# One PSUM bank moved from the transpose pool to the projection pool of a hybrid attention kernel

## Chip, core and metric

The kernel runs on one core of a Trainium2 chip, in one launch. The metric is the time on the device in microseconds (us). TensorE is called PE below, VectorE DVE, ScalarE ACT, GpSimd POOL; SyncE (SP) issues the transfers. [...]

## What is computed

One block with two branches over 2048 tokens of width 1024, float32, cut to what matters:

```python
h = rmsnorm(x, norm_g)
proj = einsum("bsd,de->bse", h, w_in)
glu_in, conv_gate, q, k, v, attn_gate, merge_logits = split(proj, SPLIT_POINTS)
c = conformer_conv(glu_in, ...)        # a * sigmoid(b), 31 taps per channel, layernorm, silu
y_conv = (c * silu(conv_gate)) @ w_conv_out
q, k = rope(q), rope(k)                # 16 query heads, 4 key heads of 64
a = sliding_window_attention(q, k, v, sinks)     # window 128
y_attn = (a * silu(attn_gate)) @ w_attn_out
g_conv, g_attn = split(sigmoid(merge_logits))
x = x + (g_conv * y_conv + g_attn * y_attn) @ w_out
return rmsnorm(x, final_norm_g)
```

## The kernel before

The tokens go through in two sweeps of 1024 (`sweep`). Activations lie transposed in SBUF (channels on partitions), each as a high and a low half of reduced precision, and a product is the sum of three: high by high, high by low, low by high.

`project` (L267) makes an item: one block of 128 output channels for the two halves of 512 tokens of the sweep. `load_w` (L244) fetches the weight block in two parts: a transfer into `raw`, a cast on ACT into `whi` (L253), and the low part `wlo` as a subtraction on POOL (L242, `split_lo`), or in the second sweep as a transfer of the stored low part. Per half, 24 matmuls (8 blocks of input channels by 3) go into one PSUM tile `mm_<name>` from the pool `mm_ps` (L276). `evac` then reads that tile out, with a raised priority (L284, L285): items gb by a sigmoid on ACT (L415), ga by a product on DVE (L419), the gates cg, ag, ma and mc on ACT (L434), q and k by four rope products on DVE (L460, L461 of item a, L466, L467 of item b), whose sums POOL makes (L468, L469) and ACT splits (L296), v on ACT (L519). A tile's bank is free for a later tile when its last reader has ended.

The pool `tp_ps` holds the tiles of transposes and of weighted values, one bank each: tpf (`build_h_first`, the transposed first activations, 8 tiles for each half of the first sweep; read by ACT at L363 and by DVE at L364), tpx (`build_h`, the second sweep), tpv (values, L497; read by ACT at L501 and L513 and by DVE at L502, L503 and L242), tpp (probabilities of the attention, L592, read by ACT at L599 and by DVE) and ov (weighted values, L610, read by ACT at L617 and DVE at L618). [...] 

The order of PE is the program's own: it is written out by hand, with the class `Line` placing attention steps, value transposes and convolution taps between the blocks of the projection items. The other engines are put in order by a scheduler that goes by priorities and by when it thinks operands are ready. The convolution's 31 taps for each of 8 channel blocks and each sweep run on DVE (L389, L393, 128x1024 each) beside the projections. The first sweep begins with tpf, gb and ga of the first block, k, v and q (to about 220 us), goes on with gb, ga and gates, and has the attention among them up to about 630 us; then come the gates ma and mc, the output projections, and the second sweep.

Of the kernel before, what the change touches and what calls it, by code (L numbers as in the profile page):

```python
# [53 lines left out]
def hybrid_block(ctx: ExitStack, tc: tile.TileContext, x, par_d, w_in, w_conv, sinks, w_attn, w_out,  # L54
# [5 lines left out]
    slots = ctx.enter_context(tc.tile_pool(name="slots", bufs=1))  # L60
    stage = ctx.enter_context(tc.tile_pool(name="stage", bufs=4))
    work = ctx.enter_context(tc.tile_pool(name="work", bufs=2))
    mm_ps = ctx.enter_context(tc.tile_pool(name="mm_ps", bufs=3, space=bass.MemoryType.PSUM))
    tp_ps = ctx.enter_context(tc.tile_pool(name="tp_ps", bufs=3, space=bass.MemoryType.PSUM))
    sc_ps = ctx.enter_context(tc.tile_pool(name="sc_ps", bufs=1, space=bass.MemoryType.PSUM))
    dram = ctx.enter_context(tc.tile_pool(name="dram", bufs=1, space=bass.MemoryType.DRAM))

# [889 lines left out]
```

## Time and profile before

| what | us |
|---|---|
| median of 3 runs | 2091.1 (2090.81 to 2091.75) |
| profiled execution, its own time | 2090.34 |
| its span, first to last instruction | 2088.4 |
| PE busy | 2044.0 |
| DVE busy | 1391.3 |
| ACT busy | 1032.4 |
| POOL busy | 483.2 |
[...]

The span is the profiled execution without 1.9 us around it. PE is busy for all but 44 us of it, and all its idle time of more than a trifle lies before 632 us. Three ways of reading the trace are used below. The waits of an engine name, for idle time, the line that sat idle and the instruction that ended the idleness. Busy time by stretch shows which engine has no idle time in a part of the span, and the clock that was granted there. The timeline lists single instructions or runs of equal ones, with the idle time ahead of each in brackets.

### The profile page before, as it was taken

What the parts mean: (1) busy time and instruction counts of PE and PEld (TensorE: products, weight loads), DVE (VectorE), ACT (ScalarE), POOL (GpSimd) and SP (SyncE); (2) the same over time, 40 slices, a digit from 0 to 9 for tenths busy, and PEclk for the clock granted to TensorE, in tenths of its full rate; (3) what the DMA queues carried; (4) which work ended last, traced back from release to release, by engine and by line L of the source; (5) the groups of instructions that cost most, each with busy time, mean ns of one, the idle gap of its engine ahead of it and who ended that gap; (6) DMA issues with size and microseconds to landing.
All of it is one profiled execution on the core that took longest, in us unless ns stands there. A gap on an engine that the chain in (4) does not pass through costs nothing.

```text
span 2088.4 us, 27452 instructions
## 1 busy us (share of the span) xinstructions
PE 2044.0 (98%) x9256; PEld 1671.7 (80%) x9256; DVE 1391.3 (67%) x1901; ACT 1032.4 (49%) x2265; POOL 483.2 (23%) x336
## 2 busy tenths in 40 slices
PE   7999999998999999999999999999999999999998
PEld 6787888886777888888888888888888888888887
DVE  4979779998988348123559596698888934341324
ACT  6221377666667646112442214766777774621222
POOL 2445433433334222243001131121111110000200
PEclk9999999999999999999999999999999999999999
DMA  7344555554455775646344456555555578574432
GB/s 250 133 144 157 178 166 157 158 163 146 148 152 182 254 238 184 202 142 221 101 151 132 141 161 204 172 158 175 175 163 164 175 225 259 162 236 146 140 119 81
DMA packets 265820, 355.90 MB, mean 170 GB/s; under 512 B 28112, under 2 KB 126544, under 8 KB 265680
## 3 DMA queue, kind: packets, MB, share of 16 engines
q1 hardware_dynamic: 265680, 354.16, 53.3%
q8 instruction: 73, 1.20, 0.2%
q14 instruction: 67, 0.55, 0.1%
HBM read 234.51 MB, written 119.54 MB: 170 GB/s over the span
## 4 chain that ended last, share of the span: by engine, by line
PE 70%; DVE 4%; issue 2%; ACT 1%; DMA 0%; POOL 0%; SPq 0%; DVEq 0%; POOLq 0%; ACTq 0%
PE o L877 9%; PE mm_mc L281 8%; PE mm_yc L281 8%; PE mm_ya L281 8%; PE mm_ma L281 7%; PE mm_ga L281 5%; PE mm_cg L281 5%; PE mm_ag L281 4%; PE mm_gb L281 4%; DVE cv L393 2%; PE mm_q_a L281 2%; PE mm_q_b L281 2%; PE ov L614 2%; PE sc L566 2%; PE mm_v L281 1%
## 5 line engine op out<-in xcount | busy, mean ns | idle before, releaser
L393 DVE SCALAR_TENSOR_TENSOR cv<-glu,par,cv 128x1024 f32<-128x1024 f32 x480 | 675.9, 1408 | 6.7
L605 POOL TENSOR_SCALAR_AFFINE_SELECT pc<-pt 128x1024 fp32r<-128x1024 f32 x60 | 102.7, 1711 | 452.9 <-DVE pt L242 419.6
L877 PE MATMUL o<-wo,mT 128*128 128x512 f32 x768 | 181.3, 394 | 0.0
L877 PEld LDWEIGHTS o<-wo,mT 128*128 128x128 f32 x768 | 143.1, 188 | 32.1
L281 PE MATMUL mm_cg<-hT,whi_cg 128*128 128x512 f32 x512 | 163.2, 400 | 4.6 <-ACT glu L415 3.0
L281 PE MATMUL mm_ma<-hT,whi_ma 128*128 128x512 f32 x512 | 162.9, 399 | 4.0 <-ACT whi_ma L253 4.0
L281 PE MATMUL mm_ga<-hT,whi_ga 128*128 128x512 f32 x512 | 161.0, 395 | 0.2 <-ACT whi_ga L253 0.2
L281 PE MATMUL mm_ag<-hT,whi_ag 128*128 128x512 f32 x512 | 160.9, 395 | 0.0
L281 PE MATMUL mm_gb<-hT,whi_gb 128*128 128x512 f32 x512 | 160.6, 395 | 0.0
L281 PE MATMUL mm_mc<-hT,whi_mc 128*128 128x512 f32 x512 | 159.6, 393 | 0.0
L281 PE MATMUL mm_yc<-uT,whi_yc 128*128 128x512 f32 x512 | 159.4, 392 | 0.0
L281 PE MATMUL mm_ya<-aT,whi_ya 128*128 128x512 f32 x512 | 158.7, 391 | 0.0
L281 PEld LDWEIGHTS mm_cg<-hT,whi_cg 128*128 128x128 f32 x512 | 95.3, 191 | 25.2 <-ACT glu L415 3.4
L281 PEld LDWEIGHTS mm_ma<-hT,whi_ma 128*128 128x128 f32 x512 | 95.1, 190 | 23.9 <-ACT whi_ma L253 4.4
L281 PEld LDWEIGHTS mm_yc<-uT,whi_yc 128*128 128x128 f32 x512 | 96.2, 188 | 21.9
L281 PEld LDWEIGHTS mm_mc<-hT,whi_mc 128*128 128x128 f32 x512 | 96.0, 188 | 21.8
L281 PEld LDWEIGHTS mm_ya<-aT,whi_ya 128*128 128x128 f32 x512 | 96.1, 188 | 20.9
L281 PEld LDWEIGHTS mm_ga<-hT,whi_ga 128*128 128x128 f32 x512 | 94.5, 188 | 20.8 <-ACT whi_ga L253 1.0
L281 PEld LDWEIGHTS mm_gb<-hT,whi_gb 128*128 128x128 f32 x512 | 94.7, 188 | 20.0
L281 PEld LDWEIGHTS mm_ag<-hT,whi_ag 128*128 128x128 f32 x512 | 94.2, 188 | 19.7 <-ACT whi_ag L253 0.3
L584 ACT ACTIVATE ss<-ss,st 128x128 f32<-128x128 f32 x256 | 99.9, 391 | 19.2 <-DVE st L579 18.6
L815 POOL TENSOR_TENSOR lmc<-lmc,mp 128x512 f32<-128x512 f32 x32 | 41.9, 1309 | 275.5 <-DVE lmc L814 267.1
(363 smaller groups left out, 4356.4 us busy)
## 6 DMA issues: line engine op xcount, KB each, us to landing
qk<-d_q SPq DMA_DIRECT2D x256, 64.0 KB, 2.7
d_a<-ss SPq DMA_DIRECT2D x128, 128.0 KB, 1.9
aT<-d_a SPq DMA_DIRECT2D x32, 512.0 KB, 6.1
qk<-d_k SPq DMA_DIRECT2D x240, 64.0 KB, 2.1
raw_gb<-in_w_in_dram SPq DMA_DIRECT2D x34, 256.0 KB, 4.0
raw_ga<-in_w_in_dram SPq DMA_DIRECT2D x34, 256.0 KB, 3.4
raw_ag<-in_w_in_dram SPq DMA_DIRECT2D x32, 256.0 KB, 3.8
d_ag<-ag SPq DMA_DIRECT2D x32, 256.0 KB, 2.1
```

What stands on the lines that cost most here:

```text
L281: pe.matmul(out=ps, lhsT=a, rhs=b, start=(k == 0 and i == 0), stop=(k == KC - 1 and i == 2))
L393: dve.scalar_tensor_tensor(out=cv[c], in0=glu[c][:, j:j + T], scalar=tap(c, j), in1=cv[c], op0=ALU.mult, op1=ALU.add)
L566: pe.matmul(out=o, lhsT=q[:, h, :], rhs=r, start=(j == 0), stop=(j == 1))
L584: act.activation(out=sb[:, h, :], in_=sb[:, h, :], func=AF.Exp, scale=SCALE, bias=ngm[:, h:h + 1], accum_out=den[:, h:h + 1])
L605: pool.affine_select(out=pc, in_=f(pt), pattern=[[0, 2], [0, GQ], [1, P]], compare_op=ALU.is_ge, fill=0.0, base=0, channel_multiplier=-1)
L614: pe.matmul(out=ov, lhsT=vv, rhs=pp[:, i % 2], start=(i == 0), stop=(i == nm - 1))
L815: pool.tensor_tensor(out=g, in0=g, in1=mp[e][:, half * TH:(half + 1) * TH], op=ALU.add)
L877: pe.matmul(out=ps, lhsT=a[:, c0:c0 + P], rhs=r, start=(k == 0 and i == 0), stop=(k == KC - 1 and i == 2))
```

## The change

The pool of projection tiles gets four buffers instead of three, the pool of transposes and weighted values two instead of three. Nothing else is edited.

```diff
-    mm_ps = ctx.enter_context(tc.tile_pool(name="mm_ps", bufs=3, space=bass.MemoryType.PSUM))
-    tp_ps = ctx.enter_context(tc.tile_pool(name="tp_ps", bufs=3, space=bass.MemoryType.PSUM))
+    mm_ps = ctx.enter_context(tc.tile_pool(name="mm_ps", bufs=4, space=bass.MemoryType.PSUM))
+    tp_ps = ctx.enter_context(tc.tile_pool(name="tp_ps", bufs=2, space=bass.MemoryType.PSUM))
```

In both kernels the tiles of a pool take its banks in turn. The order of PE and POOL is the same instruction for instruction; DVE, ACT and SP differ only in the first 35 us or so. On ACT, at the start, hT is the copy of a tpf tile, sqf the square of an input block of the second half, whi the cast of a weight block:

```order
 L363 ACTIVATE hT_0_2_126<-tpf_2_192,par 128x512
-L363 ACTIVATE hT_0_3_127<-tpf_3_199,par 128x512
 L253 CAST whi_gb_000_139<-raw_gb_000_137 128x512
 L253 CAST whi_gb_001_145<-raw_gb_001_143 128x512
+L363 ACTIVATE hT_0_3_127<-tpf_3_199,par 128x512
 L363 ACTIVATE hT_0_4_128<-tpf_4_206,par 128x512
+L350 ACTIVATE sqf_0_235,ssf_234<-xf_0_149 128x1024
 L363 ACTIVATE hT_0_5_129<-tpf_5_213,par 128x512
-L350 ACTIVATE sqf_0_235,ssf_234<-xf_0_149 128x1024
-L363 ACTIVATE hT_0_6_130<-tpf_6_220,par 128x512
 L351 ACTIVATE ssf_234<-ssf_234,eps_t 128x1
 L350 ACTIVATE sqf_1_240,ssf_234<-xf_1_151 128x1024
```

The copies of tiles 3, 5 and 6 now stand behind two casts and one square each. The last copy has moved further, behind all four squares:

```order
-L363 ACTIVATE hT_0_7_131<-tpf_7_227,par 128x512
+L363 ACTIVATE hT_0_6_130<-tpf_6_220,par 128x512
 L351 ACTIVATE ssf_234<-ssf_234,eps_t 128x1
 L350 ACTIVATE sqf_2_245,ssf_234<-xf_2_153 128x1024
 L350 ACTIVATE sqf_3_250,ssf_234<-xf_3_155 128x1024
 L351 ACTIVATE ssf_234<-ssf_234,eps_t 128x1 x2
+L363 ACTIVATE hT_0_7_131<-tpf_7_227,par 128x512
 L253 CAST whi_ga_000_257<-raw_ga_000_255 128x512
```

On PE the order stands, and what an instruction waits for changes. At the third tile of transposed values (tpv_1_0; vs is the ACT copy of the projected values) before had

```order
L281 MATMUL mm_v_792<-hT_1_7_320,whi_v_665 128x512 x2
L281 MATMUL mm_v_792<-hT_1_7_320,wlo_v_666 128x512
L281 MATMUL mm_q_a_858<-hT_0_0_124,whi_q_a_730 128x512 x2
L281 MATMUL mm_q_a_858<-hT_0_0_124,wlo_q_a_731 128x512 [waits Pool_49]
L499 MATMUL tpv_1_0_862<-ident_r,vs_1_0_790 128x128 [waits Activation_49]
L499 MATMUL tpv_1_0_862<-ident_r,vs_1_0_790 128x128 x3
```

and after has

```order
L281 MATMUL mm_v_792<-hT_1_7_320,whi_v_665 128x512 x2
L281 MATMUL mm_v_792<-hT_1_7_320,wlo_v_666 128x512
L281 MATMUL mm_q_a_858<-hT_0_0_124,whi_q_a_730 128x512 x2
L281 MATMUL mm_q_a_858<-hT_0_0_124,wlo_q_a_731 128x512 [waits Pool_49]
L499 MATMUL tpv_1_0_862<-ident_r,vs_1_0_790 128x128 [waits DVE_49]
L499 MATMUL tpv_1_0_862<-ident_r,vs_1_0_790 128x128 x3
```

The wait for ACT has become one for DVE: the tile takes the bank of the first tpv tile, whose last reader is on DVE (L242).

## Rows read from the trace of the kernel before

**Rows 1.** Waits of PE: engine, tile, line, releaser: us, times, longest.

```profile
PE mm_ma L281 <- ACT whi_ma L253: 4.0, 1, 4.0
PE mm_q_b L281 <- DVE rb_q__1_1524 L467: 3.4, 1, 3.4
...
PE mm_cg L281 <- ACT glu L415: 3.0, 1, 3.0
...
PE mm_cg L281 <- ACT cg L434: 1.7, 1, 1.7
...
PE mm_q_b L281 <- DVE ra_q__0_1408 L461: 1.3, 1, 1.3
...
PE mm_q_b L281 <- DVE ra_q__0_1579 L461: 0.5, 1, 0.5
```

**Rows 2.** Stretches: length, busy time of each engine, granted clock, DMA share, GB/s.

```profile
139.00:213.00 74.00, 68.78 (x290) 55.13 (x289) 72.84 (x61) 10.38 (x18) 33.57 (x21) 0.98 0.45 143
...
636.00:2086.00 1450.00, 1445.64 (x6537) 1186.16 (x6535) 854.73 (x1250) 687.12 (x1499) 237.36 (x164) 1.00 0.55 174
...
91.80:96.00 4.20, 2.09 (x12) 1.81 (x12) 4.20 (x8) 2.53 (x7) 0.00 (x0) 1.00 0.00 0
198.83:202.24 3.41, 3.41 (x9) 2.63 (x9) 3.27 (x3) 1.29 (x3) 2.71 (x2) 0.50 0.48 150
...
628.91:635.74 6.83, 5.72 (x13) 3.93 (x14) 6.77 (x8) 3.78 (x9) 4.72 (x3) 0.50 0.21 47
```

The engines stand in the order PE, weight load of PE, DVE, ACT, POOL.

**Rows 3.** Waits of DVE from 235 to 632 us, as in rows 1.

```profile
DVE st L586 <- ACT ss L584: 15.5, 9, 4.8
...
DVE glu L419 <- PE mm_ga L281: 4.9, 1, 4.9
```

**Rows 4.** Timeline of PE at the start: start, us, instruction, idle before.

```profile
11.77 5.84 PE L361 MATMUL tpf<-ident_r,xf 128*128 128x128 f32 x25 [0.89 <-DVE xf L354]
18.11 0.66 PE L361 MATMUL tpf<-ident_r,xf 128*128 128x128 f32 x4 [0.50 <-DVE hT L364]
18.52 0.70 PE L281 MATMUL mm_gb<-hT,whi_gb 128*128 128x512 f32 x2
...
24.45 0.73 PE L281 MATMUL mm_ga<-hT,whi_ga 128*128 128x512 f32 x2 [0.21 <-ACT whi_ga L253]
25.87 0.50 PE L281 MATMUL mm_ga<-hT,wlo_ga 128*128 128x512 f32 x1 [0.70 <-POOL wlo_ga L242]
```

**Rows 5.** Timeline of DVE at the start.

```profile
13.01 2.46 DVE L364 SCALAR_TENSOR_TENSOR hT<-tpf,par,hT 128x512 fp32r<-128x512 f32 x3 [1.29 <-ACT hT L363]
```

**Rows 6.** Timeline of ACT at the start.

```profile
12.28 0.69 ACT L363 ACTIVATE hT<-tpf,par 128x512 fp32r<-128x512 f32 x1 [1.55 <-PE tpf L361]
...
15.55 1.13 ACT L253 CAST whi_gb<-raw_gb 128x512 fp32r<-128x512 f32 x2
...
17.73 1.06 ACT L350 ACTIVATE sqf<-xf 128x1024 f32<-128x1024 f32 x1
```

**Rows 7.** Timeline of PE, later places.

```profile
93.93 0.66 PE L499 MATMUL tpv<-ident_r,vs 128*128 128x128 f32 x4 [2.11 <-ACT vs L519]
...
223.22 0.62 PE L281 MATMUL mm_ga<-hT,whi_ga 128*128 128x512 f32 x2
223.68 0.39 PE L281 MATMUL mm_ga<-hT,wlo_ga 128*128 128x512 f32 x1
...
502.44 0.60 PE L594 MATMUL tpp<-ident_r,ss 128*128 128x128 f32 x4
```

**Rows 8.** Timeline of DVE, later places.

```profile
95.68 0.42 DVE L242 TENSOR_TENSOR vt<-tpv,vt 128x256 fp32r<-128x256 f32 x1
...
138.60 0.69 DVE L419 TENSOR_TENSOR glu<-mm_ga,glu 128x512 f32<-128x512 f32 x1 [4.90 <-PE mm_ga L281]
```

**Rows 9.** Timeline of POOL around 220 us.

```profile
219.09 1.30 POOL L242 TENSOR_TENSOR wlo_ga<-raw_ga,whi_ga 128x512 fp32r<-128x512 f32 x1 [1.30 <-issue]
```

**Rows 10.** Timeline of ACT in the attention.

```profile
519.30 0.58 ACT L599 CAST pt<-tpp 128x512 fp32r<-128x512 f32 x1
```

## The prediction, made before the changed kernel ran

> **What bounds the kernel now.** I read the waits of TensorE (PE) first, because PE has little idle time to give back: whatever the change brings must be one of those waits. The rows to look at are the five in which a projection tile (an "mm" tile) waits for the reader of an older mm tile: VectorE (DVE) rope lines L467 and L461, ScalarE (ACT) lines L415 and L434. They come to 3.4 + 1.3 + 0.5 = 5.2 us in the rope stretch and 3.0 + 1.7 = 4.7 us in the attention stretch [rows 1]. These are true buffer waits: the reader holds the tile three back, which is the bank that the next tile wants. The row for mm_ma (4.0 us, for the cast of a weight block, at the end of the attention stretch) is not one; a buffer does nothing for it.
>
> Then the busy time by stretch. From 139 to 213 us DVE is busy 72.84 of 74 us, more than PE. [...] From 636 us on PE is busy 1445.64 of 1450 us: it alone sets the pace there, and a shift of the 632 us before stays a shift of the end [rows 2].
>
> Last, who paces 235 to 632 us. The waits of DVE there have one row for PE, 4.9 us, and all others for ACT, 15.5 us ahead [rows 3]. So DVE and ACT run a chain of their own that PE doesn't hold up, and PE is their customer.
>
> **The change part by part: two transpose buffers at the start.** The order of PE and of GpSimd (POOL) stays word for word. Each of the eight tpf tiles takes four transposes of 0.234 us, 0.93 us in all (5.84 us for 25) [rows 4], then an ACT copy and a DVE subtraction that ends the tile's life. On DVE three of these took 2.46 us, so 0.75 us and some for each [rows 5]; the ACT copy is 0.69 us [rows 6]. With three buffers PE lost 0.50 us once, before the last tile at 18.11 [rows 4]. With two, tile k+2 starts when DVE has done with tile k: 0.93 + 0.69 + 0.75 and two hand-overs, some 2.5 us for two tiles, where PE alone needs 1.9. Besides, ACT's order now has the two weight casts (1.13 us) ahead of hT3 and the 1.06 us square ahead of hT5 [rows 6], as the order of the changed kernel shows. Walking through: tile 2 at 13.8, tile 3 at 14.7, tile 4 at 16.4 (behind hT2 on DVE), tile 5 at 18.0 (hT3 behind the casts), tile 6 at 18.9, tile 7 at 20.5 (hT5 behind the square); mm_gb begins at about 21.3 instead of 18.52, +2.8. hT7 now stands behind all four squares on ACT and comes free of DVE at about 26.1, just ahead of mm_gb's last three matmuls at 26.3. Against this, PE lost 0.21 + 0.70 us at the next item, mm_ga, waiting for weights, with 0.11 twice in slower first matmuls, a pair in 0.73 and a single in 0.50 [rows 4], where 0.62 and 0.39 are usual [rows 7]; a later PE finds those weights there: −1.1. So +1.7 at full clock. The clock rose at about 17.9 before. With gaps between the transposes it rises with mm_gb or one stretch of 3.4 us later: 0 to 1.6 us; I take the middle, 0.8. Sum: +2.5, bounds 1.7 and 5.
>
> **Two transpose buffers at the value tiles.** At 93.93 the third tpv tile waited 2.11 us for ACT's copy of its input [rows 7]. With two buffers it takes the bank of the first tpv tile, whose last reader, DVE's L242, ends at 95.68 + 0.42 = 96.10 [rows 8]. That is 2.2 us later; queued behind the transpose on PE is the whole of mm_q_a, so all of it is lost. The idle becomes 4.3 us, and the two rows of half clock follow idles of 3.4 and 4.0 us; a stretch of 3.41 us at half clock costs 1.7. Sum: +3.9, bounds 2.2 and 5.1 (5.8 us at half clock). The two costs pass on: DVE waited 4.90 us for PE at 138.60, right ahead of its saturated stretch [rows 8], so it starts that stretch as late as PE does.
>
> [...] Without any cost of clock the sum would be the second rival's.
>
> **A fourth projection buffer, rope stretch.** It removes the 5.2 us, and the stretch of half clock behind the 3.4 us (1.7 us). But PE then comes 6.9 us earlier to mm_ga, which it met at 223.22, with the low half of the weights at 223.68 [rows 7]. That low half is POOL's at 219.09 to 220.39 [rows 9], behind ACT's cast of the same weights. Both stand behind the last step of the rope chain of the saturated DVE, which a buffer doesn't speed up. So PE gets 223.68 − 220.39 = 3.3 us, about 3.2 with the hand-over, and the rest turns into idle there, 3.7 us in two parts. Such an idle may halve the clock: 0 to 1.7, and I take half, 0.8. Gain: 2.4, bounds 1.5 and 3.2. What PE gains it passes on, since DVE waits for PE 4.9 us more, for the second half of this mm_ga [rows 3].
>
> **A fourth projection buffer, attention stretch.** The 4.7 us go as PE waits, but the end of the stretch is the cast of whi_ma that mm_ma waits for [rows 1], at the end of the DVE and ACT chain. PE would wait there for as much longer. Cost and gain nothing; if the chain were not the limit, −4.7 and −1.7 for the clock (third rival).
>
> **Two transpose buffers in attention.** Five tpp and ov tiles, from 442 to 506 us, start there before the last reader of the tile two back has ended: by the starts and ends of these in the trace 0.7, 1.9, 1.3, 3.1 and 1.8 us, 8.8 in all. I cost them at nothing. The worst, the tpp tile of 502.44 [rows 7], is read by ACT only at 519.30 [rows 10], so ACT doesn't wait for it, and PE has the 4.7 us and the 4.0 ahead of mm_ma as cover. Without that cover it is +8.8.
>
> After 636 us nothing covers a delay, but none arises either: PE shows no buffer wait there, and of the transpose tiles none starts less than 1.9 us after the last reader of the one two back.
>
> **Sum**: 2.5 + 3.9 − 2.4 = +4.0 us on the profiled execution's 2090.3 us, 2094.3. The median of the runs is 0.8 us above the profiled one, so 2095.1 us.
>
> **The rivals.** First, slower: the clock. The place is the tpv tile at 93.93. If the 4.3 us idle is followed by half clock as long as that of 628.91 to 635.74 (5.8 us of work, 2.9 lost), with the start's clock one stretch late (1.6) and the idle at mm_ga halving it too (gain only 1.5): 1.7 + 1.6 + 5.1 − 1.5 = +6.9, 2098.0. For it: the 4.0 us idle, nearest in length to 4.3, had 6.83 us [rows 2]. Against it: the 3.4 us one had 3.41. It decides from an idle of about 4 us on.
>
> Second, unchanged: no cost of clock anywhere. 1.7 + 2.2 − 3.2 = +0.7, 2091.8. For it: after the 2.11 us wait of 93.93 the clock stayed high (1.00) [rows 2]. Against it: the two rows of half clock.
>
> Third, faster: all mm waits come back, 5.2 + 1.7 and 4.7 + 1.7 = 13.3, against 6.4 of cost: −6.9, 2084.2. It holds if PE, not the DVE and ACT chain, sets the start of that mm_ma. Against it: DVE waits for PE once in 235 to 632 us [rows 3], and whi_ma is late by 4.0 us already. [...]
>
> Fourth, slower: the 8.8 us of attention shortfalls count, because what ACT reads is late after all: 2103.9. It decides if a tpp tile is read within some 3 us of being written; at 502.44 it is 17.
>
> Fifth: the change doesn't do what it says, since a tile's release comes later than its last reader's end, and buffer waits stay: within 1 us of 2091.1.
>
> **How the numbers follow.** Forecast 2095.1 (2093.4 to 2096.8): 0.42. First rival 0.24, second 0.20, third 0.06, fourth 0.05, fifth 0.03. A measurement of this kernel tells 0.2% from no change, that is 4.2 us: 2086.9 and 2095.3. The forecast's cases lie on both sides of the upper one, 0.25 within and 0.17 above. Faster 0.06; within 0.25 + 0.20 + 0.03 = 0.48; slower 0.17 + 0.24 + 0.05 = 0.46. The range goes from the second rival's 2091.8, with 0.6 below it, to the first's 2098.0 with 0.5 above: 2091.2 to 2098.5. It leaves out the third and fourth rivals and the tails of the others, under 2 in 10.
>
> **What would show it.** In the profile after: mm_gb's first matmul at 21 to 22 us instead of 18.52 (start); the third tpv at 93.93 + 2.5 + 2.2 = 98.6, with an idle of about 4.3 us that names DVE vt L242, and half clock behind it; no wait of mm_q_b for DVE, but PE waiting for whi_ga or wlo_ga at about 222 to 225; no mm_cg wait for ACT L415 or L434, and a longer idle ahead of mm_ma near 634. From there PE without waits, and the end as late as that. It would be wrong if mm_gb starts below 20, if the tpv wait doesn't grow, or if mm_ma after attention comes earlier than before.

## The result, and the profile after

The changed kernel takes 2094.32 us (median of 22 runs) against 2091.06 of the kernel before (22 runs): ratio 1.0014, interval 1.0008 to 1.002. That is 3.3 us slower, clear of the noise but below the 0.2% that the prediction drew as its line. The profiled execution took 2094.78 us, with a span of 2092.9 against 2088.4. The forecast was 2095.1 with a range of 2091.2 to 2098.5.

Waits of PE after the change; columns as in [rows 1].

```profile
PE tpp L594 <- DVE pt L242: 4.9, 3, 2.7
PE tpv L499 <- DVE vt L242: 4.4, 1, 4.4
PE mm_ma L281 <- ACT whi_ma L253: 4.0, 1, 4.0
...
PE ov L614 <- DVE ss L618: 2.5, 2, 1.3
PE tpf L361 <- DVE hT L364: 2.4, 4, 0.7
...
PE mm_gb L281 <- DVE ra_q__0_1579 L461: 1.7, 1, 1.7
```

The five buffer waits of [rows 1] are gone. In their place stand waits of transposes and weighted values for readers on DVE (tpp, tpv, ov, tpf), and a buffer wait of another projection has come up, mm_gb for a rope product. The wait of mm_ma stands as it was, 4.0 us.

PE at the start, answering [rows 4].

```profile
18.08 2.18 PE L361 MATMUL tpf<-ident_r,xf 128*128 128x128 f32 x8 [0.50 <-DVE hT L364]
20.76 1.12 PE L361 MATMUL tpf<-ident_r,xf 128*128 128x128 f32 x4 [0.50 <-DVE hT L364]
21.53 1.20 PE L281 MATMUL mm_gb<-hT,whi_gb 128*128 128x512 f32 x2
22.53 0.63 PE L281 MATMUL mm_gb<-hT,wlo_gb 128*128 128x512 f32 x1
...
24.23 1.01 PE L281 MATMUL mm_gb<-hT,whi_gb 128*128 128x512 f32 x2
25.08 0.39 PE L281 MATMUL mm_gb<-hT,wlo_gb 128*128 128x512 f32 x1
```

mm_gb begins 3.0 us later than before, and its first matmuls take 0.63 us instead of 0.39, until 25.08.

PE at the later places, answering [rows 7].

```profile
99.38 0.66 PE L499 MATMUL tpv<-ident_r,vs 128*128 128x128 f32 x4 [4.41 <-DVE vt L242]
...
100.48 0.63 PE L281 MATMUL mm_q_a<-hT,wlo_q_a 128*128 128x512 f32 x1
...
213.72 0.70 PE L281 MATMUL mm_gb<-hT,whi_gb 128*128 128x512 f32 x2 [1.70 <-DVE ra_q__0_1579 L461]
...
226.16 0.73 PE L281 MATMUL mm_ga<-hT,whi_ga 128*128 128x512 f32 x2 [1.12 <-ACT whi_ga L253]
227.58 0.50 PE L281 MATMUL mm_ga<-hT,wlo_ga 128*128 128x512 f32 x1 [0.68 <-POOL wlo_ga L242]
...
510.77 0.66 PE L594 MATMUL tpp<-ident_r,ss 128*128 128x128 f32 x4 [2.73 <-DVE pt L242]
...
635.06 0.73 PE L281 MATMUL mm_ma<-hT,whi_ma 128*128 128x512 f32 x2 [3.99 <-ACT whi_ma L253]
```

The third tpv waits 4.41 us, and slow matmuls follow. From 213 to 228 us three waits stand where none stood: 1.70, 1.12 and 0.68 us.

DVE at those places, answering [rows 8], and POOL, answering [rows 9].

```profile
98.91 0.41 DVE L242 TENSOR_TENSOR vt<-tpv,vt 128x256 fp32r<-128x256 f32 x1
...
145.70 0.69 DVE L419 TENSOR_TENSOR glu<-mm_ga,glu 128x512 f32<-128x512 f32 x1 [4.90 <-PE mm_ga L281]
```

```profile
226.24 1.28 POOL L242 TENSOR_TENSOR wlo_ga<-raw_ga,whi_ga 128x512 fp32r<-128x512 f32 x1 [1.30 <-issue]
```

The product at L419 comes 7.10 us later than before, with the same wait for PE ahead of it; wlo_ga comes 7.15 us later. DVE's chain has taken over PE's delay whole.

Stretches, columns as in [rows 2].

```profile
21.53:25.08 3.55, 3.55 (x10) 2.79 (x9) 2.46 (x7) 3.55 (x10) 0.00 (x0) 1.00 0.33 126
...
99.38:102.80 3.42, 3.42 (x12) 2.80 (x13) 3.42 (x8) 2.95 (x8) 1.14 (x1) 0.61 0.00 0
100.16:103.57 3.41, 3.41 (x10) 2.63 (x9) 3.41 (x6) 3.23 (x9) 1.91 (x2) 0.50 0.00 0
...
640.00:2086.00 1446.00, 1446.00 (x6540) 1186.60 (x6538) 854.38 (x1247) 687.31 (x1498) 237.32 (x164) 1.00 0.54 175
```

From 640 us on PE is never idle, so a shift stands to the end. The granted clock was 0.50 for 3.41 us after the tpv (third row); a stretch at 0.50 is called low clock below. At the start the row reads 1.00, but only because the trace has no entry for the clock there: its list of granted clocks begins with full clock at 25.07 us in the changed kernel and at 17.93 in the kernel before, and a stretch ahead of the first entry is counted as full. The slow matmuls end at that same 25.07: single ones take 0.63 us until then, as at 100.48 under a granted clock of 0.50, and 0.39 from 25.08 on. From this I read that the clock rose there; no entry shows it low before.

The waits of DVE from 235 to 636 us, answering [rows 3], have hardly changed:

```profile
DVE st L586 <- ACT ss L584: 15.5, 9, 4.7
...
DVE glu L419 <- PE mm_ga L281: 4.8, 1, 4.8
```

Since the order of PE is the same instruction for instruction, the starts of the same matmul in two traces can be subtracted. Shift of PE against the kernel before, in us, at five times of that kernel (the two kernels with the value transposes put later have the same matmuls in nearly the same order; e labels are the experiments below):

| kernel | 50 | 150 | 207 | 224 | 640 |
|---|---|---|---|---|---|
| changed | 3.2 | 7.1 | −0.3 | 4.0 | 4.5 |
| e1_tp2 | 3.1 | 7.4 | 7.4 | 7.4 | 7.3 |
| e2_start | 0.3 | 4.6 | −2.8 | 1.6 | 1.5 |
| e3_tpv | 3.9 | 5.5 | −1.9 | 2.4 | 1.8 |
| e4_both | 0.2 | 1.8 | −5.6 | −1.3 | −1.0 |
| e5_attn | −0.6 | 1.0 | 1.0 | 1.0 | −0.1 |
| e6_later | −0.6 | −2.9 | −9.3 | −5.0 | −4.6 |
| e7_rope_taps | −0.2 | −0.1 | −7.7 | 0.0 | −0.4 |
| e9_att_taps | 0.0 | 1.6 | −5.8 | −1.5 | −1.7 |
| e10_csum | −0.8 | −0.7 | −8.1 | −5.6 | −4.4 |
| e11_csum_taps | −0.4 | 1.1 | −6.5 | −4.3 | −5.4 |
| e12_att_taps2 | 0.2 | 1.7 | −5.7 | −1.3 | −4.8 |
| e13_later_csum | 0.4 | −1.9 | −8.3 | −5.8 | −5.8 |

The changed kernel's row tells it by place: 3.2 us lost at the start, 3.9 at the values, 7.4 won in the rope stretch, 4.3 of these lost again until mm_ga, 0.5 more lost in the attention. Each row is one execution. The other kernels with the same attention (e2, e3, e4, e6 and e7) step by −0.6 to +0.4 us from 224 to 640 us, so a step of 0.5 there says little.

### The profile page after: what moved, and what is told of

Its sections match the earlier page's. It is cut to its first block, busy times and chain, and to the rows that moved or that the text cites. A ratio compares the mean times of both kernels' runs of the same rounds, so it can differ in the third digit from the quotient of the medians.

```text
span 2092.9 us, 27511 instructions
## 1 busy us (share of the span) xinstructions
PE 2044.9 (98%) x9256; PEld 1671.8 (80%) x9256; DVE 1393.2 (67%) x1901; ACT 1032.1 (49%) x2265; POOL 482.8 (23%) x336
## 4 chain that ended last, share of the span: by engine, by line
PE 77%; DVE 13%; ACT 3%; issue 3%; DMA 1%; POOL 1%; SPq 0%; DVEq 0%; ACTq 0%; POOLq 0%
PE o L877 8%; PE mm_mc L281 8%; PE mm_yc L281 8%; PE mm_ya L281 8%; DVE cv L393 8%; PE mm_ma L281 7%; PE mm_ga L281 6%; PE mm_gb L281 6%; PE mm_ag L281 6%; PE mm_cg L281 5%; PE mm_q_a L281 3%; PE mm_q_b L281 3%; PE sc L566 2%; PE ov L614 2%; PE mm_v L281 1%
```

## Experiments

Theory: the two transpose buffers cost at the start and at the third value tile only; the projection buffer wins in the rope stretch only, and DVE's chain with POOL's weights takes half of it back. Rivals: other waits count, or PE is the limit everywhere.

Times below are medians, with the ratio to runs of the kernel before on the same chip; the kernel before was at 2090.92 (e1 to e4), 2091.04 (e5 to e9) and 2091.39 (e10 to e13). Where two experiments are compared by medians, each is first set against its own runs of the kernel before. The intervals of e4, e6 and e10 reach some 1.8 us to either side and overlap, so differences of 2 or 3 us between such experiments rest on the waits and the shifts in the table, of one execution each.

**Half of the change alone**, three projection buffers with two transpose buffers:

```diff
-    mm_ps = ctx.enter_context(tc.tile_pool(name="mm_ps", bufs=4, space=bass.MemoryType.PSUM))
+    mm_ps = ctx.enter_context(tc.tile_pool(name="mm_ps", bufs=3, space=bass.MemoryType.PSUM))
```

> Half of the change alone: two transpose buffers, projection buffers left at three. Theory: the costs stand without the gain. The start is 3.3 us late at mm_ga and the third tpv tile adds 2.1 of idle and 1.5 of half clock, 6.9 in all, and DVE is as late as PE at 140 us, so the three mm_q_b waits for DVE (5.2 us) are all still there and mm_ga near 230 is late by 7: median about 2098, 2097 to 2099.5. Rival, the waits of the tpp and ov tiles in the attention count too: 2101 to 2107. Rival, the delay is swallowed by the old waits before 632 us: 2092 to 2095.

2097.55, ratio 1.0033 (1.002 to 1.0045). The cost stands without the gain: 6.6 us by the medians, and a shift of 7.3 to 7.4 us from 150 us to the end. The attention adds nothing to it.

**The start undone.** Two of the eight tiles from the other pool give the start three banks (buffers) again:

```diff
-            tp = tp_ps.tile([P, 4, P], F32, tag="tp", name=f"tpf{half}_{k}")
+            tp = (mm_ps if half == 0 and k % 3 == 2 else tp_ps).tile([P, 4, P], F32, tag="mm" if half == 0 and k % 3 == 2 else "tp", name=f"tpf{half}_{k}")
```

> The changed kernel with its start as before: the tpf tiles 2 and 5 of the first half come from the projection pool, and every engine's order is word for word that of before. Theory: the start cost 3.3 us and passes on whole: 3.3 below the changed kernel, 2091.0 (2090 to 2092). mm_gb begins at 18.5 us, mm_ga as before; the tpv idle of 4.4 us stays. Rival, the start's delay is swallowed later (by the waits for weights near 228 us): no difference, 2094.3.

2091.99, ratio 1.0007 (0.9998 to 1.0016); at 50 us the shift is 0.3 instead of 3.2, and the difference is kept to the end (1.5 against 4.5). By the medians it is 2.2 us below the changed kernel, where 3.3 were expected.

**The value tile undone.**

```diff
-                tp = tp_ps.tile([P, 4, P], F32, tag="tp", name=f"tpv{s}_{i}_{half}")
+                tp = (mm_ps if (s, i, half) == (0, 1, 0) else tp_ps).tile([P, 4, P], F32, tag="mm" if (s, i, half) == (0, 1, 0) else "tp", name=f"tpv{s}_{i}_{half}")
```

> The changed kernel with one tile moved: the third tpv tile comes from the projection pool, so it doesn't wait for the first one's last reader. Theory: it cost 2.1 us of idle and 1.5 of half clock, which pass on: 3.6 below the changed kernel, 2090.7 (2089.7 to 2091.7); the clock stays high after the tile. Rival, only the idle counts and the half clock is made up in the later wait for DVE: 2092.2. Rival, swallowed: 2094.3.

2089.82, ratio 0.9997 (0.9989 to 1.0006): the idle is 2.1 us again and the tile doesn't wait for its bank. But "the clock stays high" didn't hold in the profiled execution, the slowest of the eleven (2092.18): there was low clock for 3.41 us, and the shift grows by 1.6 from 50 to 150 us.

**Both undone** (the two edits together): the fourth projection buffer alone.

> The changed kernel without both costs (tpf tiles 2 and 5 and the third tpv tile from the projection pool): the fourth projection buffer alone, with every engine's order as before. Theory: mm_q_b doesn't wait any more and PE runs up to 6.9 us ahead, but wlo_ga still comes at 220.4 at the end of the rope chain of the saturated DVE, so 3.2 us are left at mm_ga, and the attention stretch gives nothing: 2087.8 (2087 to 2089). Rival, PE is the limit and all mm waits with their half clock come back, 13.3 us: 2078. Rival, nothing is left, since DVE and ACT set every stage to 632 us: 2091.

2088.63, ratio 0.9987 (0.9978 to 0.9995): 2.3 us faster than before, 3.2 expected. In the profile, again the slowest of eleven runs, it is 1.0; here the granted clock fell after the 2.1 us idle, to 0.59 on the mean of 93.90 to 97.50 us, where it was 1.00 in the profile of before [rows 2]:

```profile
93.90:97.50 3.60, 3.40 (x11) 2.85 (x12) 3.60 (x8) 1.74 (x6) 0.00 (x0) 0.59 0.00 0
```

That cost 1.6 us by the table (0.2 to 1.8). From there on PE wins 7.4 us to 207 and keeps 3.1 at 224, as in the changed kernel, with the same waits at mm_ga:

```profile
220.87 0.73 PE L281 MATMUL mm_ga<-hT,whi_ga 128*128 128x512 f32 x2 [1.17 <-ACT whi_ga L253]
222.28 0.50 PE L281 MATMUL mm_ga<-hT,wlo_ga 128*128 128x512 f32 x1 [0.68 <-POOL wlo_ga L242]
```

**Attention only.** Three and two buffers, with both edits above, so that only later tiles have a bank less:

> Three projection buffers and two transpose buffers, with tpf tiles 2 and 5 and the third tpv tile taken from the projection pool: against the kernel before only the later tpf, tpv, tpp, ov and tpx tiles have a bank less, and every engine's order is that of before. Theory: their waits (8.8 us of shortfall in the attention) have cover on PE, since DVE and ACT set the end of that stretch: 2091 (2090 to 2092), with PE waiting for DVE at tpp and ov tiles of 442 to 506 us and less at mm_cg and mm_ma. Rival, what exceeds the 4.7 us of old buffer waits counts: 2095. Rival, all counts: 2100.

2091.47, ratio 1.0005 (0.9996 to 1.0014). Its waits of PE:

```profile
PE tpp L594 <- DVE pt L242: 3.3, 2, 2.7
...
PE ov L614 <- DVE ss L618: 2.5, 2, 1.3
```

5.8 us of new waits, and no loss. The two waits of mm_cg for ACT L415 and L434 [rows 1], 4.7 us, are gone here with three projection buffers too: PE, held at the tiles, comes later to them. The shift of 1.0 us at 224 became −0.1 at 640, and 0.8 at the end through a short wait for ACT near 1790. (The 1.0 is two short waits near 100 us that the value tile in the pool of three caused.) With e4_both this also says what the fourth projection buffer is worth in the attention: nothing that shows, as the shift from 224 to 640 changes by −1.1 with three and by +0.3 with four.

**The value transposes later**, with the start undone:

```diff
-                yield 0.0, 7.0
+                yield 0.0, (14.0 if s == 0 and i == 1 else 7.0)
```

> The changed kernel with the start as before and the two transposes of the second value block put later in the order of PE (12 blocks of a projection instead of 6 or so), so that neither the copy of their input nor the bank is waited for. Theory: the idle ahead of the third tpv tile (2.1 in the kernel before, 4.4 in the changed one) goes, with the half clock behind it, and DVE waits for PE that much less before its saturated stretch: 2.1 to 3.6 below the kernel with both costs undone (2088.6), so 2086.5 (2085 to 2087). Rival, it only moves a wait: 2088.6 or more.

2086.02, ratio 0.9978 (0.9969 to 0.9986), 2.7 us below e4_both by the medians and 3.6 by the table. Where the third value tile stood, no wait and no low clock is left (PE without idle from 90.32 to 93.22 us, its single matmuls 0.39 us each), and PE is 2.9 us ahead at 150, all the way through DVE's chain to the end.

**Less DVE work ahead of the rope chain:**

```diff
-                dve.scalar_tensor_tensor(out=cv[c], in0=glu[c][:, j:j + T], scalar=tap(c, j),
-                                         in1=cv[c], op0=ALU.mult, op1=ALU.add)
+                n_ = 32 if (s, c) == (0, 1) and 20 <= j < 24 else T; dve.scalar_tensor_tensor(out=cv[c][:, 0:n_], in0=glu[c][:, j:j + n_], scalar=tap(c, j),
+                                         in1=cv[c][:, 0:n_], op0=ALU.mult, op1=ALU.add)
```

> The kernel with both costs undone, and with four taps of channel block 1 (of those that DVE does from 140 to 210 us) done on 32 instead of 1024 columns, which leaves out that part of the convolution: some 5 us less for DVE ahead of the rope chain. Theory: DVE's chain, through POOL's wlo_ga, takes 4 of PE's 7 us back at mm_gb and mm_ga; with the chain 5 us earlier they stay: 4 below 2088.6, 2084.6 (2083.5 to 2086), and PE doesn't wait for wlo_ga near 222. Rival, the buffers were all that held PE: 2088.6.

2089.86, ratio 0.9996 (0.9987 to 1.0005): a miss of 5 us. The waits at mm_ga went, as expected, but one of 4.04 us came up at mm_gb. POOL first, then PE:

```profile
206.36 2.35 POOL L399 TENSOR_TENSOR csum<-csum,cv 128x1024 f32<-128x1024 f32 x1 [5.05 <-DVE cv L393]
208.67 1.26 POOL L242 TENSOR_TENSOR wlo_gb<-raw_gb,whi_gb 128x512 fp32r<-128x512 f32 x1
```

```profile
209.98 0.80 PE L281 MATMUL mm_gb<-hT,wlo_gb 128*128 128x512 f32 x1 [4.04 <-POOL wlo_gb L242]
```

With shorter taps the scheduler put POOL's sum of the channel block (csum) ahead of wlo_gb; POOL sat 5.05 us for the block's last tap, with PE's weights queued behind. In e4_both csum stood behind them, but ahead of the last rope sums:

```profile
214.57 2.42 POOL L399 TENSOR_TENSOR csum<-csum,cv 128x1024 f32<-128x1024 f32 x1 [6.37 <-DVE cv L393]
...
217.08 1.31 POOL L468 TENSOR_TENSOR ra_q__0_1579<-ra_q__0_1579,rb_q__0_1652 128x512 f32<-128x512 f32 x1
...
220.94 1.28 POOL L242 TENSOR_TENSOR wlo_ga<-raw_ga,whi_ga 128x512 fp32r<-128x512 f32 x1 [1.30 <-issue]
```

So the run showed a suspect that the theory had missed: POOL's order may take the gain back as well as DVE. Two later runs test it.

**Less DVE work in the attention**, the same edit for block 5 on the kernel with both costs undone:

> The kernel with both costs undone, and with four taps of channel block 5 (done by DVE between 440 and 510 us) on 32 instead of 1024 columns, which leaves out that part of the convolution: some 5 us less for DVE. Theory: DVE and ACT, not PE and its buffers, set the end of the attention stretch, so all of it is gained: 5 below 2088.6, 2083.6 (2082.5 to 2085). Rival, PE sets it, DVE's time there is hidden: 2088.6. Rival, ACT alone sets it: 2087 to 2088.6.

2088.17, ratio 0.9985 (0.9976 to 0.9994): almost nothing, a miss. But this edit had also changed the order on ACT, with the cast at L621 now ahead of the sigmoid at L415, and DVE waited for what came behind:

```profile
514.86 0.16 DVE L586 TENSOR_TENSOR st<-st 128x4 f32<-128x4 f32 x1 [4.23 <-ACT ss L584]
```

That wait is about as long as the cut. So the run doesn't tell the theory from its rivals.

**POOL's sum later:**

```diff
-                    if not conv_done:
-                        pool.tensor_copy(out=csum, in_=cv[c])
-                    else:
+                    if not conv_done: pool.tensor_copy(out=csum, in_=cv[c])
+                    elif (s, c) != (0, 1):
                         pool.tensor_tensor(out=csum, in0=csum, in1=cv[c], op=ALU.add)
+                        if (s, c) == (0, 2): pool.tensor_tensor(out=csum, in0=csum, in1=cv[1], op=ALU.add)
```

> The kernel with both costs undone, and POOL's sum of channel block 1 (csum, 2.4 us) done after that of block 2 instead of ahead of the last rope sums near 215 us. Theory: POOL starts those sums when DVE's rope products are there, 1.8 us earlier, wlo_ga and PE's mm_ga come 1.8 us earlier: 2087.0 (2086 to 2088), with a shorter wait of PE for whi_ga and wlo_ga near 220. Rival, DVE alone holds wlo_ga back: 2088.6.

2086.81, ratio 0.9979 (0.997 to 0.9988), 2.3 us below e4_both by the medians, 1.7 by the ratios. Its POOL and PE:

```profile
212.75 1.30 POOL L468 TENSOR_TENSOR ra_q__0_1579<-ra_q__0_1579,rb_q__0_1652 128x512 f32<-128x512 f32 x1 [0.47 <-DVE rb_q__0_1652 L466]
```

```profile
217.97 0.51 PE L281 MATMUL mm_ga<-hT,wlo_ga 128*128 128x512 f32 x1 [0.27 <-POOL wlo_ga L242]
```

POOL now waits for DVE, and PE's 1.17 and 0.68 us at mm_ga in e4_both are down to 0.27. From 150 to 224 us the kernel wins 4.9 us instead of 3.1, the 1.8 that were expected.

**The sum later and four early taps of block 1 cut:**

> As the run before, and with taps 4 to 7 of channel block 1 (near 150 us on DVE) on 32 instead of 1024 columns, which leaves out that part of the convolution; so the rope chain ends 4 us earlier and POOL has no sum queued ahead of the weights of mm_gb. Theory: nothing takes back what the buffers gave PE in the rope stretch: 4 below the kernel with both costs undone (2088.6), 2084.6 (2083.5 to 2086), no wait at mm_gb and mm_ga. Rival, the 4 us of DVE don't matter: as the run before.

2085.45, ratio 0.9972 (0.9961 to 0.9983), 1.4 us below the run before, not 2.2. The wait at mm_ga is gone, one of 1.85 us at mm_gb for wlo_gb isn't: on POOL a small copy for the next block, which waits 5.03 us for DVE's last tap, stands ahead of wlo_gb. From 150 to 224 the gain is 5.4 us of the 7.6 that the buffers brought by 207. So the shorter taps added 0.5 us to that of e10_csum, with DVE's rope products and POOL's queue in another order. What holds back the rest, DVE's time or these queues, stays open.

**Taps of block 6 cut**, 570 to 580 us, on the kernel with both costs undone:

> The kernel with both costs undone, and with taps 22 to 25 of channel block 6 (570 to 580 us on DVE) on 32 instead of 1024 columns, which leaves out that part of the convolution. Theory: from 523 to 630 us the order of DVE sets the pace, taps and attention steps in one queue, and the copy of taps in the middle of it took the gain of the earlier cut away through a changed order on ACT: here 4 us of DVE bring about 4: 2084.5 (2083.5 to 2086). Rival, hand-overs between DVE and ACT set the pace and a tap is filling: 2088 or so.

2083.04, ratio 0.9963 (0.995 to 0.9975). Against e4_both that is 3.8 us by the table, 5 by the ratios and some 6 by the medians of only five runs, which lie below the range expected. PE at mm_ma:

```profile
625.52 0.73 PE L281 MATMUL mm_ma<-hT,whi_ma 128*128 128x512 f32 x2 [1.40 <-ACT whi_ma L253]
```

mm_ma comes 4.1 us earlier than in e4_both (629.65), about as much as the cut took from DVE. But this run too changed the order of the other engines between 572 and 591 us: on POOL, csum stood behind a step of the attention and the weights of mm_ga and mm_ma in e4_both (first line), and stands ahead of them here (second line).

```profile
588.18 2.53 POOL L399 TENSOR_TENSOR csum<-csum,cv 128x1024 f32<-128x1024 f32 x1 [1.63 <-DVE cv L393]
579.49 2.41 POOL L399 TENSOR_TENSOR csum<-csum,cv 128x1024 f32<-128x1024 f32 x1 [8.87 <-DVE cv L393]
```

A wait of PE for wlo_gb near 569 us grew from 0.65 to 3.00 us and didn't stop mm_ma from coming earlier. So the end moved when DVE had less to do, and not with PE's waits; how much of it is DVE's time and how much the new order isn't told apart.

**The best of them**, transposes later and POOL's sum later:

> The kernel with the start as before and the second value block's transposes later (2086.0), and POOL's sum of channel block 1 after that of block 2. Theory: both gains add, since DVE waits for PE behind the values and PE waits for POOL behind the rope: 1.8 below, 2084.2 (2083.2 to 2085.5). Rival, no gain from the sum: 2086.0.

2084.68, ratio 0.9969 (0.9957 to 0.9982): 6.7 us faster than the kernel before, some 10 than the changed one. Against e6_later that is 1.7 us by the medians and 1.2 by the table, where 1.8 were expected, so the two gains nearly add up.

## Why the prediction was right, point by point

**Start.** Forecast +2.5 us, measured 3.2 [rows 4]. The walk through the tiles was right to a few tenths: mm_gb at 21.5 (21.3 forecast), the last copy behind four squares, the waits at mm_ga gone (0.21 + 0.70 us). The slow first matmuls cost 1.6 us, the upper end, where I had taken 0.8; that they were the clock's is read from their 0.63 us, as under 0.50 at 100.48, and from the clock's first entry, 1.00 at 25.07 us. That gaps between the transposes put the clock's rise off was my estimate: the first entry came 7.1 us later, but that the gaps did it is not shown. The upper bound of 5 us had no working behind it.

**Values.** Forecast +3.9, measured 3.9: an idle of 4.41 us that names L242, 2.3 more than before, and 3.41 us of low clock behind it. e3_tpv confirms what the bank did to the idle.

**Rope stretch.** Forecast −2.4, measured −3.1 (7.1 to 4.0). Two things differed. I had let the idle ahead of mm_ga halve the clock with an even chance; it came as 1.70, 1.12 and 0.68 us, and the granted clock stayed at 1.00 behind them (from 103.57 to 557.54 us). And 1.70 of it is a buffer wait of mm_gb, which I hadn't foreseen: PE runs so far ahead that four buffers are too few as well. That wlo_ga behind the rope chain takes part of it back was right; that the saturated DVE [rows 2] is the cause is not shown. e10_csum shows POOL's csum, in the queue between DVE's last product and the rope sums, to hold 1.8 us of it. Of the rest no run gives DVE its share, since e7_rope_taps and e11_csum_taps changed POOL's queue too.

**Attention.** Forecast nothing, measured +0.5 in the profile, hardly more than single executions differ by. e5_attn shows both halves: its 5.8 us of tile waits cost nothing, and the fourth buffer brings nothing there. One sign failed: I had expected a longer idle ahead of mm_ma, and it is 3.99 us as before. PE didn't carry the 4.7 us of mm_cg to that place; the waits of tpp and ov (7.4 us in all, 8.8 forecast) took their place on the way, and that of mm_cg for wlo_cg grew from 2.0 to 3.2 us. So the gain and the cost that I had each put at nothing, with that idle as cover, largely took each other's place before mm_ma. The reason for the nothing, DVE and ACT as the pace [rows 3], is supported for 560 to 630 us by e12_att_taps2, with the order changed beside it, and left open for 440 to 520, where e9_att_taps changed ACT's order. Where the 0.5 may come from is seen partly: from 235 to 252 us DVE's shift grows from 4.0 to 4.7 us, where other operations of DVE took longer than in the kernel before (below).

**The sum against the median.** The profiles differ by 4.4 us, where 4.0 were forecast, and the medians by 3.3. That the sum came so near is in part luck: the 0.7 us missing at the start and the 0.7 missing from the rope gain cancel. What came in too much is the last step, the 0.8 us by which the median of before lay above its profile: the profile of the changed kernel lies 0.5 above its median. Each profile is one execution out of a spread of 2.9 us (before, 2089.67 to 2092.57) or 3.4 us (changed, 2092.58 to 2096.02), so an offset of this size belongs to the execution that was profiled. One part of it is seen: of nine profiles with an idle of 2.1 to 2.2 us at the third value tile, five had low clock behind it (e3, e4, e9, e11, e12) and four had not (before, e5, e7, e10), a difference of 1.6 us; all three with 4.3 to 4.4 us (changed, e1, e2) had it. But that isn't what makes the spread: the changed kernel spreads no less, and e6_later, which has no idle there, runs from 2085.24 to 2088.55. Where most of it comes from stays open.

**Rivals.** The first (longer low clock) didn't come in the changed kernel: 3.4 us of work at low clock behind the 4.4 us idle, where the rival had 5.8. It wasn't far, as e1_tp2 and e2_start had 4.4 and 4.5 us of it behind the same idle. The second (no cost of clock) was wrong at both places. The third fell with e4_both, 2088.6 and not 2078. The fourth fell with e5_attn and e1_tp2, and the fifth with the five waits gone. The time didn't follow those waits, as the forecast had it: 2.3 us of 9.9 came back in e4_both.

## What to carry over

A buffer moved from one pool to another is to be priced in both pools, tile by tile: for the one that loses it, by the start of each tile against the last reader of the tile that will then be in its bank; for the one that wins it, by the next thing that PE meets when it comes early (here weights queued behind another engine's chain, 3 us of 7 left). Where the loss sits in two tiles, these can be given a bank of the other pool, or be placed later, and the gain is kept. And an experiment that shortens work under a scheduler can change queues too, as all four did here: its order has to be compared before its time is read.

## What the hardware showed unexpectedly

An idle of PE of 2.1 to 2.2 us at the third value tile was followed by low clock in some profiles and not in others: in five of nine, at 1.6 us each. The kernel before had such a case of its own, which the prediction didn't use: an idle of 1.96 us at 553.80 us, and behind it

```profile
553.82:557.23 3.41, 3.41 (x8) 2.73 (x9) 3.35 (x6) 0.99 (x3) 1.90 (x1) 0.50 0.69 224
```

So its clock of 1.00 after the 2.11 us wait [rows 2] was one of the two outcomes seen.

After the sparser transposes the first matmuls took 0.63 us instead of 0.39 for 3.5 us, the same durations as behind the 4.4 us idle, where the granted clock was 0.50. The clock's first entry in the trace, 1.00, comes at 25.07 to 26.20 us in the three kernels with the changed start (changed, e1, e3) and at 15.20 to 18.23 us in the other eleven. In the changed kernel four transposes ahead of that entry took 1.12 us (20.76); in the kernel before 25 took 5.84 us ahead of it, and four 0.66 behind it [rows 4]. Under a granted clock of 0.50 four took 1.05 us (522.02 in the kernel before), and under 1.00 0.60 [rows 7]. So the 1.00 in that row is no measurement; that the clock was low there is my reading of these durations.

In each of the two profiles a 128x4 operation of DVE that ran beside POOL's subtractions took some 1.1 us longer than the same one elsewhere; in the kernel before, POOL's took longer too. The kernel before, DVE first and POOL second:

```profile
241.36 1.25 DVE L579 SCALAR_TENSOR_TENSOR st<-st,nsink 128x4 f32<-128x4 f32 x1
```

```profile
238.53 4.06 POOL L242 TENSOR_TENSOR wlo_ag<-raw_ag,whi_ag 128x512 fp32r<-128x512 f32 x2 [9.64 <-ACT whi_ag L253]
```

Two subtractions on POOL took 4.06 us (one of the same shape 1.30 at 219.09 [rows 9]), and a 128x4 operation of DVE within them 1.25 us, where the median of the 64 at L579 is 0.154 us (the changed kernel at 244.94: 0.16). In the changed kernel the long one was L581 at 246.26, 1.26 us (0.15 at 243.75 in the kernel before), inside POOL's 246.02 to 248.75; POOL's two subtractions took 2.73 us there. So in these two profiles, some 4 us apart there, the long operation is not the same, and DVE's own shift changes by some tenths; whether the end follows isn't shown. That they coincide is seen; what they share wasn't tested.
